# Moving the products, the split weights and one exponential around two RMSNorms of a two-layer trunk

## The chip, the cores and the metric

The kernel runs on one core of a Trainium2 chip. The core has a matrix engine (TensorE, PE, with a weight load PEld that overlaps it), a vector engine (VectorE, DVE), a scalar engine for activations and copies (ScalarE, ACT), a general engine (GpSimd, POOL) and a queue that issues the large transfers (SyncE, SP). Each engine works through its own instructions in order and waits for others by semaphores. The metric is the device time of one execution in microseconds (us): the median of the executions of one kernel. Lower is better.

## The reference

A trunk of two layers works on 256 tokens of width 2048 in float32. Layer 0 mixes tokens with a Conformer convolution, layer 1 with a Mamba-2 state-space mixer (64 heads in 8 groups); behind each mixer stands a squared-ReLU MLP with 8192 hidden columns. A norm with a modulation from a conditioning vector stands ahead of each of the four.

```python
for i in range(DEPTH):
    mod = (sc @ w_mod[i] + b_mod[i])[:, None, :]
    sh1, sc1, g1, sh2, sc2, g2 = jnp.split(mod, 6, axis=-1)
    u = rmsnorm(h, norm_mix_g[i]) * (1 + sc1) + sh1
    ...
    h = h + g1 * mix
    u = rmsnorm(h, norm_mlp_g[i]) * (1 + sc2) + sh2
    h = h + g2 * sq_relu_mlp(u, mlp_w1[i], mlp_w2[i])
return rmsnorm(h, final_norm_g)

def sq_relu_mlp(u, w1, w2):
    h = jax.nn.relu(u @ w1)
    return (h * h) @ w2

def mamba2(u, w_in, conv_w, conv_b, dt_bias, a_log, d_skip, norm_g, w_out):
    zxbcdt = u @ w_in
    z = zxbcdt[..., :D_INNER]
    xbc = zxbcdt[..., D_INNER:D_INNER + MB_CONV_CH]
    dt_raw = zxbcdt[..., D_INNER + MB_CONV_CH:]
    ...
    dt = jax.nn.softplus(dt_raw.astype(jnp.float32) + dt_bias.astype(jnp.float32))
    A = -jnp.exp(a_log.astype(jnp.float32)).reshape(MB_GROUPS, MB_HPG)
    y = ssd_chunked(xs, dt, A, Bm, Cm) + d_skip.reshape(MB_GROUPS, MB_HPG)[..., None] * xs
    ...

def ssd_chunked(xs, dt, A, Bm, Cm):
    ...
        acum = jnp.cumsum(dtc * a_f, axis=1)
        seg = acum[:, :, None] - acum[:, None, :]
        decay = jnp.exp(jnp.where(tril, seg, -jnp.inf))
    ...
```

## The kernel before

The stream `h` lies turned in the core's memory: columns of the model on the 128 partitions, the 256 tokens along a row, in four groups of four tiles (`h_75` to `h_78`). Weights come in blocks of 1 MB, issued by SP in the order of the program (`load_w`). Each weight and each activation is split into a high part of reduced precision and a low part that holds the rest: ACT casts the high part of half a block (`wh`, L386), DVE subtracts it to get the low part (`wl`, L388), both 128x1024. A product of full accuracy is then hi*hi + hi*lo + lo*hi. PE issues these as products of 512 columns (the high weight against both parts of the activation) and of 256 (the low weight), at L417, or at L401 as single products of 256.

**A norm.** Squares of `h` are taken on ACT as the last columns are added (`square_sum`, L599; the addition is L984). `rstd_cols` adds them over the partitions with products of one column (L573), ACT takes the root (L578) and DVE the reciprocal (L579). `rstd_bcast` puts the result on a diagonal (`diag`, L548) and PE spreads it over the partitions (L553). `modulate` then works on one tile of 128x256 after another: DVE multiplies (`nrm`, L607), ACT adds the shift and casts the high part of `u` (L537), DVE makes the low part (L538). The first product needs the first tile.

**Fill.** While PE has nothing to do in a norm, it is given products of constants (`turn`, `turn_over`, L561): 3 ahead of the column sums, 5 behind them, 6 ahead of the first product (`FILL`). Each shows as two records in the profile. Where `self.held` holds products that were set aside, `turn` issues those instead. This is so in the norm ahead of the first MLP; in the norms ahead of the mixer of layer 1 and of the second MLP it is empty.

**What sets the order.** A list scheduler places each instruction by the program's order and by priorities (`high_priority`), and `issue_after(x)` keeps an instruction behind `x` in the order of its engine. Inside `outer`, which opens an MLP with the products of several blocks in turn, the second half of the first weight is split behind the last square (`self.sq`) and the diagonal (`self.dg`).

**Time steps.** In the mixer, `time_steps` multiplies `u` with the columns of `w_in` for `dt` (L1268 and L1270, 16 pairs, placed between the first blocks of `w_in`), in two halves of split weights (L1262 and L1264). It then makes softplus, the exponential of `a_log` (`na`, L1285, negated at L1286) and the cumulative sums (scans, L1305). Those go to a buffer in device memory (`ac_d`), from which `scores` reads them back over all partitions (`acc`, L1345, issued by POOL) and adds the mask (L1351, on DVE). The sum of a block's products goes into `xpad` at L1198, by which a bank of PE's output comes free, and DVE's convolution works on `xpad` at L1218.

Of the kernel before, what the change touches and what calls it, by code (L numbers as in the profile page):

```python
# [15 lines left out]
P = 128  # L16
T = 256
# [41 lines left out]
OPEN = 3  # L59
# [3 lines left out]
FILL = 16, 3, 5, 6, 8  # L63

# [124 lines left out]
class Trunk:  # L189
# [303 lines left out]
    def outer(self, srcs, make, evac, pump, there=()):  # L493
# [3 lines left out]
        for _ in range(len(self.held) or 1):  # L497
            self.turn(banks[0][0][:, :P], FILL[4] if there else FILL[3])
        there = list(there)
        for g in range(4):  # L500
            x = make(g)
            for b, src in enumerate(srcs):
# [3 lines left out]
                with self.tc.high_priority(self.ahead):  # L506
                    after = (self.hi, self.split) if done else (self.sq, self.dg) if g == 0 and b == 0 else (None, None)
                    parts = self.split_w(w, done, after)
# [34 lines left out]
    def rstd_bcast(self, sums, n):  # L543

        nc = self.nc
        r = self.rstd_cols(sums, n, FILL[1])
# [5 lines left out]
        self.turn(ps[:, :P], FILL[2])  # L552
# [12 lines left out]
    def rstd_cols(self, sums, n, fill=0):  # L565
# [3 lines left out]
        if fill:  # L569
            self.turn(ps[:, :P], fill)  # L570
        for i, s in enumerate(sums):
            for q in range(2):
                ins = nc.tensor.matmul(ps[:, q:q + 1], lhsT=s[:, q * P:(q + 1) * P], rhs=self.ones[:, :1],  # L573
                                       start=i == 0 and q == 0, stop=i == len(sums) - 1, skip_group_check=True).ins
        if fill:
            self.pe = ins
# [25 lines left out]
    def modulate(self, r, layer, sc, sh, g):  # L602

        ug = self.b("u", [P, 4, 2 * T], F32R)
        for t in range(4):
# [4 lines left out]
            self.split = self.split_x(ug, t, m, self.mod_tile(layer, sh, g)[:, t:t + 1])  # L610
        return ug
# [425 lines left out]
    def mlp(self, layer, ss, pump=None, after=None, first=None):  # L1037
        nc, a = self.nc, self.a
        with self.tc.high_priority(AHEAD_CHAIN):
            r = self.rstd_bcast(ss, D)  # L1040
# [12 lines left out]
        for c in range(4):  # L1053
# [16 lines left out]
            if c == 0:  # L1070
                self.outer([a["w1"][layer, b] for b in range(OPEN)], make, act, first or (lambda g: 0))
                if layer == 1:
                    self.todo.append(self.to_rows())
# [90 lines left out]
    def mamba(self, ss):  # L1164
# [10 lines left out]
        self.time_steps(u)  # L1175
# [73 lines left out]
    def time_steps(self, u):  # L1249
# [6 lines left out]
        self.turn_over(bank[:, :P], FILL[3], self.pe)  # L1256
        for i in range(2):
# [5 lines left out]
            with self.tc.issue_after(self.dg) if i else nullcontext():  # L1263
                nc.vector.tensor_tensor(out=wl, in0=w[:, s8, :], in1=wh.bitcast(F32), op=ALU.subtract)  # L1264
            for k in range(8):
                kt = 8 * i + k
                x = u[kt // 4]
                nc.tensor.matmul(bank, lhsT=wh[:, k, :], rhs=x[:, kt % 4, :], start=kt == 0, stop=False,  # L1268
                                 skip_group_check=True)
# [14 lines left out]
        with self.tc.issue_after(self.sq):  # L1284
# [196 lines left out]
```

## Time and profile before

| what | before |
| --- | --- |
| median of 3 runs | 2544.52 us (2544.44 to 2545.41) |
| the profiled execution, its own time | 2543.68 us |
| its span in the profile | 2541.9 us |
| granted clock of PE, mean | 0.998 |
| DVE, low parts of weights (L388) | 940.9 us in 768, 1230 ns each |
| ACT, high parts of weights (L386) | 806.4 us in 768, 1051 ns each |
| DMA | 664.31 MB, 261 GB/s mean |

The times of the profile count from the start of the span. The norm ahead of the mixer stands at 1110 us, the one ahead of the second MLP at 1812 us. In the timeline `x6` counts records that follow each other, and the name in brackets behind an arrow is what ended the idle time ahead of the row. Matmuls are pipelined, so that the length of one record is more than the distance to the next.

### The profile page before, as it was taken

Reading aid. Unit: us, or ns where it says so; the run is one execution under the profiler, and the core shown is the slowest. Engines: PE = TensorE matmul, PEld = TensorE weight load, DVE = VectorE, ACT = ScalarE, POOL = GpSimd, SP = SyncE. Lnnn points to the kernel's source line nnn. Section 1 sums busy time; section 2 is a strip of 40 time slices with the busy share of each in tenths; the row PEclk is TensorE's granted clock in tenths of the full one; section 3 lists DMA queues with packets and bytes.
Section 4 is the critical chain, followed back from the end, with each engine's and each line's share of the span. In section 5 each row is a group of like instructions: output and inputs, shape, how many; then the busy total and the mean of one; then the engine's idle time right before and its main releaser. Section 6 shows DMA issues by size and latency. Waiting matters only on the chain.

```text
span 2541.9 us, 36894 instructions
## 1 busy us (share of the span) xinstructions
PE 2514.0 (99%) x14623; PEld 2170.2 (85%) x14623; DVE 1938.1 (76%) x2524; ACT 1326.4 (52%) x2030; POOL 145.1 (6%) x201
## 2 busy tenths in 40 slices
PE   9999999999999999999999999999999999999998
PEld 7888799988888888887888888888998888888887
DVE  6799888868878888887787878898975565565565
ACT  2088654544434434457777767744454443443444
POOL 0011000000100000001000000000001101001000
PEclk9999999999999999999999999999999999999999
DMA  9998887888888878856555455788765555555554
GB/s 403 419 354 290 346 353 288 292 339 311 322 310 330 330 309 332 311 199 205 190 193 184 171 187 188 253 321 320 284 249 198 185 196 187 195 186 196 191 191 149
DMA packets 94894, 664.31 MB, mean 261 GB/s; under 512 B 10977, under 2 KB 11105, under 8 KB 16769
## 3 DMA queue, kind: packets, MB, share of 16 engines
q1 hardware_dynamic: 89138, 643.82, 68.1%
q0 software_dynamic: 5152, 16.97, 2.4%
q8 instruction: 114, 1.87, 0.3%
q10 hardware_dynamic: 432, 1.19, 0.1%
q14 instruction: 58, 0.48, 0.1%
HBM read 656.50 MB, written 2.20 MB: 259 GB/s over the span
## 4 chain that ended last, share of the span: by engine, by line
PE 89%; DVE 5%; DMA 3%; ACT 2%; issue 1%; POOL 0%; SPq 0%; DVEq 0%; ACTq 0%; POOLq 0%
PE mm L417 49%; PE mm L401 11%; PE mm L460 8%; PE mm L461 8%; PE mm L459 8%; DVE taps L688 2%; DMA hid<-wmT 2%; ACT taps L670 1%; DVE hid L316 1%; PE mm L792 1%; PE ms L1404 1%; DMA w<-open 1%; DMA wm<-wmT 1%; DVE wm L316 1%; DMA acc<-ac_d 0%
## 5 line engine op out<-in xcount | busy, mean ns | idle before, releaser
L388 DVE TENSOR_TENSOR wl<-w,wh 128x1024 fp32r<-128x1024 f32 x768 | 940.9, 1230 | 476.3 <-ACT wh L386 471.9
L386 ACT CAST wh<-w 128x1024 fp32r<-128x1024 f32 x768 | 806.4, 1051 | 929.3 <-PE mm L417 476.3
L417 PE MATMUL mm<-u,wh 128*128 128x512 f32 x3136 | 995.8, 399 | 5.5 <-DVE xpad L1198 5.3
L417 PEld LDWEIGHTS mm<-u,wl 128*128 128x128 f32 x3136 | 588.4, 188 | 139.1 <-DVE wl L388 1.1
L417 PE MATMUL mm<-u,wl 128*128 128x256 f32 x3136 | 617.5, 278 | 0.6 <-DVE wl L388 0.6
L417 PEld LDWEIGHTS mm<-u,wh 128*128 128x128 f32 x3136 | 480.4, 189 | 13.6 <-DVE xpad L1198 5.8
L459 PE MATMUL mm<-wh,hid 128*128 128x512 f32 x896 | 350.7, 391 | 0.0
L461 PE MATMUL mm<-wh,hid 128*128 128x512 f32 x896 | 348.7, 389 | 0.0
L460 PE MATMUL mm<-wl,hid 128*128 128x512 f32 x896 | 348.6, 389 | 0.0
L316 DVE SCALAR_TENSOR_TENSOR wm<-wm,scb 128x2048 f32<-128x2048 f32 x134 | 306.4, 2287 | 15.1 <-DMA wm<-wmT 14.8
L401 PE MATMUL mm<-u,wh 128*128 128x256 f32 x1408 | 254.0, 284 | 0.8 <-DVE u L538 0.8
L401 PEld LDWEIGHTS mm<-u,wh 128*128 128x128 f32 x1408 | 218.4, 192 | 3.8 <-DVE u L538 1.2
L459 PEld LDWEIGHTS mm<-wh,hid 128*128 128x128 f32 x896 | 168.2, 188 | 35.6 <-issue 1.0
L460 PEld LDWEIGHTS mm<-wl,hid 128*128 128x128 f32 x896 | 168.2, 188 | 35.3 <-issue 0.5
L461 PEld LDWEIGHTS mm<-wh,hid 128*128 128x128 f32 x896 | 168.2, 188 | 35.0
L401 PE MATMUL mm<-u,wl 128*128 128x256 f32 x704 | 196.3, 283 | 0.3 <-DVE wl L388 0.2
L417 PE MATMUL mm<-hid,wh 128*128 128x512 f32 x448 | 141.9, 398 | 0.0
L401 PEld LDWEIGHTS mm<-u,wl 128*128 128x128 f32 x704 | 133.8, 192 | 0.7 <-DVE wl L388 0.7
L316 DVE SCALAR_TENSOR_TENSOR hid<-hid,scb 128x2048 f32<-128x2048 f32 x46 | 105.4, 2290 | 19.8 <-DMA hid<-wmT 19.8
L670 ACT ACTIVATE taps<-u,par 128x256 f32<-128x256 f32 x248 | 102.4, 501 | 8.6 <-DVE u L660 5.1
L417 PEld LDWEIGHTS mm<-hid,wl 128*128 128x128 f32 x448 | 84.1, 188 | 19.7
L345 POOL TENSOR_TENSOR mod<-mod,par 128x4 f32<-128x4 f32 x40 | 38.9, 972 | 1059.3 <-DVE wm L316 898.4
(264 smaller groups left out, 2206.1 us busy)
## 6 DMA issues: line engine op xcount, KB each, us to landing
w<-w SPq DMA_DIRECT2D x256, 1024.0 KB, 4.9
wm<-wmT SPq DMA_DIRECT2D x139, 1024.0 KB, 7.3
w<-win SPq DMA_DIRECT2D x80, 1024.0 KB, 4.9
hid<-wmT SPq DMA_DIRECT2D x53, 1024.0 KB, 11.0
w<-wout SPq DMA_DIRECT2D x32, 1024.0 KB, 6.7
w<-pw SPq DMA_DIRECT2D x27, 1024.0 KB, 5.5
w<-open SPq DMA_DIRECT2D x16, 1024.0 KB, 14.1
acc<-ac_d POOLq DMA_DIRECT2D x16, 512.0 KB, 8.4
```

What stands on the lines that cost most here:

```text
L316: self.sum = nc.vector.scalar_tensor_tensor(out=w, in0=w, scalar=1.0, in1=self.scb, op0=ALU.mult, op1=ALU.mult, accum_out=m[:, i:i + 1]).ins
L345: nc.gpsimd.tensor_tensor(out=m, in0=m, in1=b, op=ALU.add)
L386: nc.scalar.copy(out=wh, in_=w[:, s, :])
L388: nc.vector.tensor_tensor(out=wl, in0=w[:, s, :], in1=wh.bitcast(F32), op=ALU.subtract)
L401: self.pe = self.nc.tensor.matmul(out, lhsT=lhsT, rhs=rhs, skip_group_check=True, **kw).ins
L417: self.pe = self.nc.tensor.matmul(out, lhsT=lhsT, rhs=rhs, start=start and not lows, stop=stop and bool(lows), skip_group_check=True).ins
L459: mm(banks[q], lhsT=hi, rhs=wh[:, k, :], start=t == 0, stop=False)
L460: mm(banks[q], lhsT=hi, rhs=wl[:, k, :], start=False, stop=False)
L461: mm(banks[q], lhsT=lo, rhs=wh[:, k, :], start=False, stop=t == NT - 1)
L670: st["tap"] = nc.scalar.activation(out=p4[:, q, :], in_=vp[:, k + q:k + q + T], func=AF.Identity, scale=self.col("w_dw", ct * TAPS + k + q ...
L688: nc.vector.tensor_add(wide, wide, products(four("wl"), k))
L792: self.pe = nc.tensor.matmul(o, lhsT=w[:, i, j * P:(j + 1) * P], rhs=u[g][:, t, :], start=ct == 0 and j < 2, stop=ct == NT - 1, skip_group ...
```

## The change

In the two norms with an empty `self.held`, the column sums stand directly behind the last products of the block ahead; the 5 fills behind the sums become 3 (`AFTER_SUMS`), the 6 ahead of the first product 4 (`TO_FIRST`). The first weight of an MLP is loaded and its first half is split ahead of the norm's chain, the low part behind the last addition to `h` (`self.evac`); the high part of the second half stands behind the last square and its low part behind the split of the second tile of `u` (`self.second`). In the mixer, the low part of the second half of the time steps' weights is placed behind the last split of the first group of `u` instead of the diagonal, and the exponential of `a_log` behind the last high part of that group instead of the last square. The first product of the time steps is issued in two halves, the one with the high parts first.

```diff
 FILL = 16, 3, 5, 6, 8
+AFTER_SUMS, TO_FIRST = 3, 4
...
-    def outer(self, srcs, make, evac, pump, there=()):
+    def outer(self, srcs, make, evac, pump, there=(), hi_after=None):
...
-            self.turn(banks[0][0][:, :P], FILL[4] if there else FILL[3])
+            self.turn(banks[0][0][:, :P], FILL[4] if hi_after is None else FILL[3] if self.held else TO_FIRST)
...
-                    after = (self.hi, self.split) if done else (self.sq, self.dg) if g == 0 and b == 0 else (None, None)
+                    after = (None, None) if not done else (hi_after, self.second) if hi_after else (self.hi, self.split)
...
-        r = self.rstd_cols(sums, n, FILL[1])
+        r = self.rstd_cols(sums, n, FILL[1], True)
...
-        self.turn(ps[:, :P], FILL[2])
+        self.turn(ps[:, :P], FILL[2] if self.held else AFTER_SUMS)
...
-    def rstd_cols(self, sums, n, fill=0):
+    def rstd_cols(self, sums, n, fill=0, chain=False):
...
-        if fill:
+        if fill and self.held:
             self.turn(ps[:, :P], fill)
-        for i, s in enumerate(sums):
-            for q in range(2):
...
+        with self.tc.issue_after(self.pe) if chain else nullcontext():
+            for i, s in enumerate(sums):
+                for q in range(2):
...
-        if fill:
+        if chain:
             self.pe = ins
...
             self.split = self.split_x(ug, t, m, self.mod_tile(layer, sh, g)[:, t:t + 1])
+            if t == 1:
+                self.second = self.split
...
     def mlp(self, layer, ss, pump=None, after=None, first=None):
         nc, a = self.nc, self.a
+        w = self.load_w(a["w1"][layer, 0][0])
         with self.tc.high_priority(AHEAD_CHAIN):
+            half = self.split_half(w, 0, None, self.evac)
             r = self.rstd_bcast(ss, D)
...
-                self.outer([a["w1"][layer, b] for b in range(OPEN)], make, act, first or (lambda g: 0))
+                self.outer([a["w1"][layer, b] for b in range(OPEN)], make, act, first or (lambda g: 0),
+                           there=[(w, [half])], hi_after=self.sq)
...
-        self.time_steps(u)
+        self.time_steps(u, rows)
...
-        self.turn_over(bank[:, :P], FILL[3], self.pe)
+        self.turn_over(bank[:, :P], TO_FIRST, self.pe)
...
-            with self.tc.issue_after(self.dg) if i else nullcontext():
+            with self.tc.issue_after(first[1]) if i else nullcontext():
                 nc.vector.tensor_tensor(out=wl, in0=w[:, s8, :], in1=wh.bitcast(F32), op=ALU.subtract)
...
-                nc.tensor.matmul(bank, lhsT=wh[:, k, :], rhs=x[:, kt % 4, :], start=kt == 0, stop=False,
-                                 skip_group_check=True)
+                for c in (slice(0, T), slice(T, 2 * T)) if kt == 0 else (slice(0, 2 * T),):
+                    nc.tensor.matmul(bank[:, c], lhsT=wh[:, k, :], rhs=x[:, kt % 4, c],
+                                     start=kt == 0 and c.start == 0, stop=False, skip_group_check=True)
...
-        with self.tc.issue_after(self.sq):
+        with self.tc.issue_after(first[0]):
             nc.scalar.activation(out=na, in_=self.col("a_log", 0)[:H], func=AF.Exp)
```

The lines of the kernel move by up to 9, so that L388 becomes L389, L538 L539, L607 L610, L1264 L1272 and L1351 L1360. The number behind a name counts buffers and differs by a few between the two kernels.

DVE in the norm ahead of the mixer, before, from the reciprocal on (`wl_9604` is the low part of the time steps' second half, `wl_9684` that of the mixer's first block, `u_9506` and `u_9523` the first two groups):

```order
L579 RECIPROCAL rcol_9494<-rcol_9494 128x2
L548 TENSOR_TENSOR diag_9497<-ident,rcol_9494 128x256
L1264 TENSOR_TENSOR wl_9604<-w_1432_9574,wh_9603 128x1024
L607 SCALAR_TENSOR_TENSOR nrm_9507<-h_75,mod_5089,ms_9499 128x256
L607 SCALAR_TENSOR_TENSOR nrm_9511<-h_75,mod_5089,ms_9499 128x256
L1286 TENSOR_SCALAR na<-na 64x1
L538 SCALAR_TENSOR_TENSOR u_9506<-nrm_9507,mod_6136,u_9506 128x256
```

and, seven rows further on:

```order
L607 SCALAR_TENSOR_TENSOR nrm_9524<-h_76,mod_5390,ms_9499 128x256
L607 SCALAR_TENSOR_TENSOR nrm_9528<-h_76,mod_5390,ms_9499 128x256
L388 TENSOR_TENSOR wl_9684<-w_1449_9681,wh_9683 128x1024
L538 SCALAR_TENSOR_TENSOR u_9523<-nrm_9524,mod_6412,u_9523 128x256
L538 SCALAR_TENSOR_TENSOR u_9523<-nrm_9528,mod_6412,u_9523 128x256
```

The same place of DVE in the changed kernel, where the first `nrm` follows the diagonal at once (left out), from the second group on:

```order
L610 SCALAR_TENSOR_TENSOR nrm_9519<-h_76,mod_5390,ms_9496 128x256
L610 SCALAR_TENSOR_TENSOR nrm_9523<-h_76,mod_5390,ms_9496 128x256
L1272 TENSOR_TENSOR wl_9598<-w_1432_9569,wh_9597 128x1024
L539 SCALAR_TENSOR_TENSOR u_9518<-nrm_9519,mod_6412,u_9518 128x256
L539 SCALAR_TENSOR_TENSOR u_9518<-nrm_9523,mod_6412,u_9518 128x256
L610 SCALAR_TENSOR_TENSOR nrm_9527<-h_76,mod_5390,ms_9496 128x256
L610 SCALAR_TENSOR_TENSOR nrm_9531<-h_76,mod_5390,ms_9496 128x256
L1295 TENSOR_SCALAR na<-na 64x1
L389 TENSOR_TENSOR wl_9678<-w_1449_9675,wh_9677 128x1024
```

The time steps' low part, the constant and the first block's low part have all moved behind the first group. On PE the 16 pairs of time-step products then end with fewer block products between them (38 of 512 and 38 of 256 before, 32 and 30 now).

DVE at the first scores, 60 us further on, before (`acc` is the tile that waits for the read of `ac_d`, `xpad` what a bank of PE's output waits for):

```order
L388 TENSOR_TENSOR wl_10117<-w_1520_10114,wh_10116 128x1024
L1218 SCALAR_TENSOR_TENSOR a_9882<-xpad,par,a_9882 128x256
L1351 TENSOR_TENSOR acc_9927<-acc_9927,mask 128x1024
L1351 TENSOR_TENSOR acc_9928<-acc_9928,mask 128x1024
L388 TENSOR_TENSOR wl_10121<-w_1520_10114,wh_10120 128x1024
L1198 TENSOR_TENSOR xpad<-mm_9893,lo_10071 128x256
```

and in the changed kernel:

```order
L1360 TENSOR_TENSOR acc_9921<-acc_9921,mask 128x1024
L389 TENSOR_TENSOR wl_10037<-w_1505_10030,wh_10036 128x1024
L1360 TENSOR_TENSOR acc_9922<-acc_9922,mask 128x1024
L389 TENSOR_TENSOR wl_10111<-w_1520_10108,wh_10110 128x1024
L389 TENSOR_TENSOR wl_10115<-w_1520_10108,wh_10114 128x1024
L1206 TENSOR_TENSOR xpad<-mm_9887,lo_10065 128x256
```

The masks have moved up past the splits of one and a half blocks.

DVE in the norm ahead of the second MLP, before (`wl_16314` and `wl_16372` are the low parts of the first two weights):

```order
L984 SCALAR_TENSOR_TENSOR h_78<-mm_15996,mod_8059,h_78 128x256
L579 RECIPROCAL rcol_16265<-rcol_16265 128x2
L548 TENSOR_TENSOR diag_16268<-ident,rcol_16265 128x256
L388 TENSOR_TENSOR wl_16314<-w_2497_16307,wh_16313 128x1024
L607 SCALAR_TENSOR_TENSOR nrm_16291<-h_75,mod_8358,ms_16270 128x256
L607 SCALAR_TENSOR_TENSOR nrm_16295<-h_75,mod_8358,ms_16270 128x256
L388 TENSOR_TENSOR wl_16372<-w_2502_16365,wh_16371 128x1024
L538 SCALAR_TENSOR_TENSOR u_16290<-nrm_16291,mod_14542,u_16290 128x256
```

and in the changed kernel (`wl_16250` is the low part of the first half of the first weight, `wl_16301` that of its second half):

```order
L989 SCALAR_TENSOR_TENSOR h_78<-mm_15990,mod_8059,h_78 128x256
L389 TENSOR_TENSOR wl_16250<-w_2481_16247,wh_16249 128x1024
L582 RECIPROCAL rcol_16262<-rcol_16262 128x2
L549 TENSOR_TENSOR diag_16265<-ident,rcol_16262 128x256
L610 SCALAR_TENSOR_TENSOR nrm_16284<-h_75,mod_8358,ms_16267 128x256
L610 SCALAR_TENSOR_TENSOR nrm_16288<-h_75,mod_8358,ms_16267 128x256
L539 SCALAR_TENSOR_TENSOR u_16283<-nrm_16284,mod_14536,u_16283 128x256
```

Nothing stands any more between the diagonal and the first split of `u`; the first weight's low part is ahead of the reciprocal.

More of the change, by code (lines that the diff above doesn't have):

```diff
@@ L563, in turn_over @@
         return ins
-    def rstd_cols(self, sums, n, fill=0):
+    def rstd_cols(self, sums, n, fill=0, chain=False):
         nc = self.nc
         ps = self.bank(self.ms, "ms")
-        if fill:
+        if fill and self.held:
             self.turn(ps[:, :P], fill)
-        for i, s in enumerate(sums):
-            for q in range(2):
-                ins = nc.tensor.matmul(ps[:, q:q + 1], lhsT=s[:, q * P:(q + 1) * P], rhs=self.ones[:, :1],
-                                       start=i == 0 and q == 0, stop=i == len(sums) - 1, skip_group_check=True).ins
-        if fill:
+        with self.tc.issue_after(self.pe) if chain else nullcontext():
+            for i, s in enumerate(sums):
+                for q in range(2):
+                    ins = nc.tensor.matmul(ps[:, q:q + 1], lhsT=s[:, q * P:(q + 1) * P], rhs=self.ones[:, :1],
+                                           start=i == 0 and q == 0, stop=i == len(sums) - 1,
+                                           skip_group_check=True).ins
+        if chain:
             self.pe = ins
@@ L1247, in mamba, with time_steps @@
         return st["ss"]
-    def time_steps(self, u):
+    def time_steps(self, u, first):
         nc, a = self.nc, self.a
```

## The prediction

> **What bounds the kernel now.** I read the page first, then what TensorE (PE) waited for, then the chain of waits and the timeline around the norms that the change touches.
>
> ```profile
> span 2541.9 us, 36894 instructions
> PE 2514.0 (99%) x14623; PEld 2170.2 (85%) x14623; DVE 1938.1 (76%) x2524; ACT 1326.4 (52%) x2030; POOL 145.1 (6%) x201
> ```
>
> PE is busy 99% of the span, so a cut on any other engine is worth only the PE idle time or the PE filler that it takes away. The waits of PE, longest in total first (line waited at, what released it, us in total, times, longest):
>
> ```profile
> PE mm L417 <- DVE xpad L1198: 5.3, 1, 5.3
> ...
> PE mm L716 <- DVE u L660: 1.6, 1, 1.6
> ...
> PE mm L401 <- DVE u L538: 0.8, 2, 0.6
> ...
> PE mm L417 <- DVE wl L388: 0.6, 1, 0.6
> ```
>
> The 5.3 us lie 40 us behind the mixer's norm, where the first scores are masked. The small ones at L401, L1268 and `wl` lie in the norms; there PE's time hides in filler (L561), which counts as busy. So the views that decide are the chain at the two norms and at that 5.3 us gap. The first MLP's norm is not part of the sum: with products still in `self.held` its branches are those of before, and its rows stand in the same order on every engine.
>
> **Norm ahead of the second MLP.** Chain of waits, start, length, what:
>
> ```profile
> 1812.45 0.67 PE ms L561 x6
> 1813.12 1.68 PE ms L573 x16
> 1814.80 1.22 PE ms L561 x10
> 1816.02 0.44 PE ms L1102 x4
> 1816.46 0.45 PE ms L553 x2
> ...
> 1817.33 0.47 DVE nrm L607
> 1817.80 1.14 DVE wl L388
> 1818.94 0.41 DVE u L538
> ...
> 1819.39 10.69 PE mm L401 x87
> ```
>
> and two rows of the timeline there:
>
> ```profile
> 1813.33 1.03 ACT L386 CAST wh<-w 128x1024 fp32r<-128x1024 f32 x1
> 1814.84 0.26 ACT L578 ACTIVATE rcol<-ms,eps 128x2 f32<-128x2 f32 x1 [0.48 <-PE ms L573]
> ```
>
> Three fills (six records) ahead of the sums go, so the sums start at 1812.45 and end at 1814.13, 0.67 earlier. The root cannot follow by all of it: the cast on ScalarE (ACT) runs to 1814.36, so it gains 0.48. PE's 3 fills (0.73) and 4 transposes (0.44) behind the sums end at 1815.30, about when `diag` is ready, so the broadcast starts near 1815.35 instead of 1816.46. The first `nrm` gains 1.0 (VectorE, DVE, is now held by `diag` and the broadcast). The `wl` of 1.14 between `nrm` and the low part of `u` is gone from that place, 0.2 of this is lost to ACT's high part: the low part starts at 1816.94 instead of 1818.85 and the first product that waits for it at 1817.46 instead of 1819.39. That is **1.9 us**. What is late next: the second half's `wl`, behind the second split; it ends before PE reaches it, since PE has 4 chunks of products with the first half (over 2 us) ahead. Behind 1819.39 PE runs without a gap, so the 1.9 us reach the end.
>
> **Norm ahead of the mixer.** The same edits, another result. Rows of its chain and of the timeline:
>
> ```profile
> 1110.50 0.67 PE ms L561 x6
> ...
> 1118.78 0.78 DVE nrm L607 x2
> 1119.56 1.14 DVE wl L388
> ...
> 1120.75 0.74 PE mm L417 x4
> 1121.49 0.23 PE mm L1268
> ...
> 1122.20 1.17 PE mm L417 x7
> 1123.37 0.23 PE mm L1268
> ```
>
> ```profile
> 1113.16 1.28 ACT L1285 ACT_TABLE_LOAD   x1
> 1113.72 1.22 DVE L1264 TENSOR_TENSOR wl<-w,wh 128x1024 fp32r<-128x1024 f32 x1
> 1116.58 0.50 PE L1268 MATMUL mm<-u,wh 128*128 128x512 f32 x1 [0.69 <-DVE u L538]
> ```
>
> The sums again start 0.67 earlier; `wl` of L1264 (1.22) is no longer ahead of `nrm`, the table load and the constant are no longer ahead of ACT's first high part, and the first product needs only the high part. I get it at 1115.19 instead of 1116.58: 1.39 gained. But nothing is removed from DVE, only moved behind, and here DVE sets the pace. Group 0's last split ends at 1117.9 (0.9 earlier); behind it come two `nrm` (0.78), the moved `wl` (1.14) and the fifth low part (0.41 in the chain above), so PE gets that at 1120.3, having run out at 1118.9. Then the sixth low part, two `nrm`, the constant and the block's `wl` (0.4 + 0.8 + 0.1 + 1.14) end at 1122.7. By then PE has done 6 pairs of time-step products (0.35 each: 0.23 for L1268 here and 0.12 for L1270 in the fence below) and 8 block products of 512 (seven products of L417, three of 512 and four of 256, took 1.17, so 0.23 and 0.12 each): 3.96 us of work in 7.49. Before it had done 5.59 us of work (6 pairs, 11 of 512, 8 of 256) by 1123.37. It will have the missing 1.63 done at 1124.31, 0.94 later than before; small waits that remain in the rows of before come off, and I take **0.7 us later**. This norm gives its gain back.
>
> **The time steps and the gap of 5.3 us.** The time steps' last product ended at 1137.25 in the chain; from there through the scans to the DMAs and the mask:
>
> ```profile
> 1137.13 0.12 PE mm L1270
> ...
> 1158.03 0.27 DVE wm L1305
> ...
> 1158.59 3.62 DMA ac_d<-wm
> ...
> 1163.42 10.73 DMA acc<-ac_d
> ...
> 1174.17 0.04 DVE acc L1351
> ...
> 1175.32 1.22 DVE wl L388
> 1176.54 0.34 DVE xpad L1198
> ...
> 1176.92 8.24 PE mm L417 x37
> ```
>
> ```profile
> 1137.17 1.05 ACT L386 CAST wh<-w 128x1024 fp32r<-128x1024 f32 x1 [1.83 <-PE mm L1268]
> ...
> 1170.89 1.22 DVE L1351 TENSOR_TENSOR acc<-acc,mask 128x1024 f32<-128x1024 f32 x1 [4.27 <-DMA acc<-ac_d]
> ```
>
> ```profile
> 1176.88:1180.15 3.27, 3.23 (x10) 2.75 (x11) 2.21 (x4) 2.40 (x8) 0.00 (x0) 0.50 1.03 343
> ```
>
> ```profile
> 275.70:279.00 3.30, 3.29 (x59) 2.34 (x63) 2.12 (x3) 1.61 (x4) 0.00 (x0) 1.00 1.03 429
> ```
>
> Between the first and the last time-step product stood 38 block products of 512 and 38 of 256; now it is 32 and 30. That is 6 x 0.23 + 8 x 0.12 = 2.3 us earlier; less the 0.7 of the norm, 1.6. ACT's copy of the result stood behind the cast of the row at 1137.17, which ended 0.97 us after the product; that cast now falls elsewhere among the products, which I put at 0.6; between there and the scans two convolution steps fewer stand on DVE. So the scans end 2.0 to 2.3 us earlier, and with the same DMA times (3.62, 10.73) both parts of `acc` arrive some **2.0 us earlier**: near 1168.8 and 1172.1.
>
> At the gap the row that PE waits for is `xpad` (L1198), and in front of it on DVE stand the mask additions, which wait for those DMAs. Before, one `wl` (1.22) stood between the second mask and `xpad`; now two do, and the first mask has moved ahead of another one. Behind the waiting masks are queued all of DVE's low parts, and PE waits for these. The second mask starts at 1172.1, and mask, `wl`, `wl` and `xpad` take 1.15 + 1.14 + 1.14 + 0.38: PE is at this row near 1176.0 instead of 1176.92, a gain of **0.9**. Its wait is no longer one of 5.29 us: it should fall into one of about 2.2 (to a `wl` behind the first mask) and two near 0.5.
>
> The last two fences (window, length, busy time of PE, PEld, DVE, ACT, POOL with counts, granted clock, DMA share, GB/s) show the clock at 0.50 for 3.27 us behind the gap, so half of that, 1.6 us, is lost; and at 1.00 behind the wait of 1.6 us at L716, which ended at 275.7. With waits of 2.2 at most I take the clock as kept: **1.6 gained**. A page speaks against taking fills out and against this step: the Trainium skill, "TensorE: Matmul & The Clock Gate", Part 1 (The HAM clock gate), has the clock halved after an idle window of about 3.4 us that runs freely. The 0.50 for 3.27 us behind a 5.29 us gap agrees with it; by that rule a gap of 2.2 us would keep the clock, two gaps that share a window might not.
>
> **Other edits.** SP and POOL issue in the same order as before, so no DMA passes another one; the exponential's table load (1.28) meets ACT while it has slack, between 0 and 1.28 late for one high part, and I take 0, since DVE is behind ACT there. Splitting one product of 512 (0.23) into two of 256 (0.12 each) costs nothing.
>
> **Sum.** -1.9 + (-0.9) + (-1.6) = -4.4; the 0.7 and the 2.3 are inside the 0.9. The profiled execution took 2543.68 us, so 2539.3 is forecast for such a one. The median of the runs, 2544.52, lies 0.84 higher, so **2540.1**.
>
> **Rivals.** (1) The clock closes all the same, in the gap (2.2 lies between the 1.6 that kept it and the 5.3 that lost it) or in the mixer's norm, where PE is busy 0.7 us between 1118.9 and 1122.7: 1.6 more, 2541.7. 18%. (2) The DMAs arrive as before, because a 1 MB weight load takes the DMA engines (share 1.03 in the row behind the gap) whenever the scans end: then the additional `wl` costs 1.1 at the gap and the clock falls as before. -1.9 + 1.1 = -0.8, 2543.7. 15%. (3) Slower: the read of `acc` is issued behind that weight load and takes 13 instead of 10.7 us (such reads took up to 13.1):
>
> ```profile
> DMA to landing us min/median/max: 4.8/8.4/13.1
> ```
>
> Each us of arrival is a us of PE; the kernel is slower than before from an arrival 0.8 us later than today's, and at 2 us later with all fills gone the sum is -1.9 + 1.1 + 2.0 = +1.2: 2545.7. 5%. (4) The arrival is over 3 us earlier, with a read of 8.4, the median: the gap nearly closes, 1.5 more, 2538.6. 15%. (5) The table load holds ACT for longer. The profile shows 1.28, started 0.02 after the root ended. If a switch cost twice that, the moved load would delay the fifth low part by 0.9 and all behind it: 2541.0. 5%. The Trainium skill, "ScalarE: Activation LUTs", What ACT_TABLE_LOAD costs, gives 1283 ns and a drain of 1380 ns, 2.66 us for a switch; no drain shows in the rows here.
>
> That the change does not do what it says is ruled out by the order of the rows shown with it.
>
> **How the numbers follow.** The forecast has 42%, with 2539.0 to 2541.3 of its own (mostly 0.7 in the mixer's norm either way). 0.2% (5.1 us) is about what a measurement of this kernel can tell from no change; faster by that means below 2539.43: rival 4 and about a third of the forecast's range, 28%. Slower by that is above 2549.6, beyond every case: 2%. The range of 8 in 10 reaches from 2537.9 (most of rival 4) to 2544.0 (rival 2), leaving out rival 3 and the edges.
>
> **What would show it.** In the profile after: the first waited product of the second MLP about 5.0 us behind the end of the block's products (6.9 before, 1812.45 to 1819.39); in the mixer's norm PE waiting about 1.4 us for `u` and 1.6 for `wl`; the write of `ac_d` about 2 us earlier against the norm's start; a wait for `xpad` under 1 us, one of 2 us a little earlier, and a granted clock of 1.00 there. A clock of 0.50 is rival 1, an unmoved arrival rival 2. The forecast is wrong where PE waits at a place that none of this names.

## The result, and the profile after

The changed kernel takes 2538.63 us (median of 9 runs, 2537.0 to 2539.75) and the kernel before 2544.86 us (9 runs, 2544.42 to 2545.66): a ratio of 0.9973 with a 95% interval of 0.9965 to 0.9981. It is 6.2 us faster, where 4.4 were forecast; the time lies in the range, 1.5 us below the forecast. The profiled execution took 2537.33 us.

The page of the changed kernel, its waits of PE and the chain of waits where the long gap was:

```profile
span 2535.5 us, 36834 instructions
...
PE 2509.7 (99%) x14596; PEld 2166.1 (85%) x14596; DVE 1937.3 (76%) x2524; ACT 1320.2 (52%) x2026; POOL 145.1 (6%) x201
```

```profile
PE mm L797 <- ACT u L791: 4.4, 12, 0.8
PE mm L251 <- DMA wm<-crow: 3.0, 1, 3.0
PE mm L721 <- DVE u L665: 1.8, 1, 1.8
...
PE mm L418 <- DVE wl L389: 1.4, 1, 1.4
...
PE mm L1277 <- DVE u L539: 1.2, 1, 1.2
```

```profile
1158.58 4.27 PE mm L418 x23
1162.85 0.49 PE ms L1343 x4
1163.34 0.11 PE ms L1348
1163.45 19.04 PE mm L418 x109
```

The wait of 5.3 us for `xpad` is gone altogether: through the first scores the chain is PE alone. In its place stand 1.2 and 1.4 us in the norm ahead of the mixer. VectorE and POOL show why (timeline; in brackets what ended the idle time):

```profile
1167.70 1.23 DVE L1360 TENSOR_TENSOR acc<-acc,mask 128x1024 f32<-128x1024 f32 x1 [2.83 <-DMA acc<-ac_d]
1168.84 1.22 DVE L389 TENSOR_TENSOR wl<-w,wh 128x1024 fp32r<-128x1024 f32 x1
1169.97 1.22 DVE L1360 TENSOR_TENSOR acc<-acc,mask 128x1024 f32<-128x1024 f32 x1
1171.11 2.35 DVE L389 TENSOR_TENSOR wl<-w,wh 128x1024 fp32r<-128x1024 f32 x2
1173.38 0.75 DVE L1206 TENSOR_TENSOR xpad<-mm,lo 128x256 f32<-128x256 f32 x2
```

The second mask no longer waits at all: its data was there before 1169.97 (its read was issued at 1160.68 and took 9.0 us).

To compare executions, the profiles are cut at two marks: A is the start of the last addition to `h` ahead of the mixer's norm, C that ahead of the second MLP's norm. These are the rows for A, of before and of after:

```profile
1110.54 0.48 DVE L984 SCALAR_TENSOR_TENSOR h<-mm,mod,h 128x256 f32<-128x256 f32 x1 [0.23 <-PE mm L401]
```

```profile
1112.12 0.48 DVE L989 SCALAR_TENSOR_TENSOR h<-mm,mod,h 128x256 f32<-128x256 f32 x1 [0.23 <-PE mm L402]
```

For C they start at 1812.49 and 1807.80. So A to C took 701.95 and 695.68 us (**-6.27**), C to the end 729.41 and 727.70 (**-1.71**), and up to A, where both kernels run the same rows, the profiled execution of after was 1.58 us slower. The table holds all kernels by these marks; times of rows are starts after A, the scans' is their end, and all are differences of rows of the profiles.

| kernel | first product | scans end | reads issued | masks 1, 2 | wait for `xpad` | A to C | C to end |
| --- | --- | --- | --- | --- | --- | --- | --- |
| before | 6.04 | 47.75 | 51.95 | 60.35, 63.63 | 5.3 | 701.95 | 729.41 |
| changed | 4.74 | 45.10 | 47.66 | 55.58, 57.85 | none | 695.68 | 727.70 |
| wl back | 4.93 | 47.16 | 51.28 | 59.35, 63.81 | 6.1 | 702.48 | 727.80 |
| exponential back | 5.00 | 45.33 | 47.88 | 55.89, 58.17 | none | 695.97 | 727.75 |
| fills back | 5.26 | 45.63 | 48.18 | 56.08, 58.36 | none | 696.21 | 728.83 |
| mixer's edits alone | 5.78 | 45.61 | 48.17 | 56.06, 58.34 | none | 696.15 | 729.41 |
| load held | 6.04 | 47.80 | 51.14 | 61.47, 66.04 | 7.7 | 704.44 | 729.40 |
| two hops | 5.39 | 47.04 | 56.91 | 65.15, 66.95 | 5.9 | 705.83 | 727.79 |
| order alone | 5.39 | 48.12 | 51.87 | 59.01, 61.99 | none | 694.81 | 727.73 |
| wl ahead of norm | 5.11 | 47.19 | 51.25 | 57.74, 62.92 | 5.1 | 702.38 | 727.68 |
| one hop | 4.74 | 45.12 | 49.95 | 56.69, 58.48 | 0.3 | 696.93 | 727.76 |
| wl early, exponential late | 4.80 | 47.62 | 51.26 | 58.53, 61.91 | none | 694.33 | 727.64 |

The stretch from C to the end agrees within 0.2 us among the kernels that are alike there, so it resolves tenths where the whole times, which spread by 0.4 to 5 us for one kernel, do not. From A to C this holds only between profiles in which the granted clock ran alike, and that differs by execution. In the mixer's norm the clock stood at 0.50 for 3.41 us in the profiles of experiments 6 to 9, from 2.6 to 3.5 us after A on, and in experiment 6 once more from 12.9. Experiment 6 (window, length, busy times of PE, PEld, DVE, ACT, POOL, granted clock, DMA share, GB/s):

```profile
1113.40:1116.80 3.40, 3.21 (x12) 2.89 (x13) 1.77 (x5) 1.31 (x3) 0.00 (x0) 0.50 0.00 0
1123.65:1127.05 3.40, 3.40 (x14) 3.11 (x15) 2.40 (x5) 2.27 (x3) 0.00 (x0) 0.50 0.37 152
```

The profile of the changed kernel has 1.00 at both places, though its rows up to 44 us after A stand in the same order as those of experiments 6 and 9. In experiment 6 the first product is therefore 0.65 and the end of the scans 1.94 us later than in the changed kernel before any copy is made. Of the eight profiles with less filler four show such a fall, of the four with the filler of before (before, 3, 4, 5) none; twelve executions do not settle whether the filler decides it.

### The profile page after: what moved, and what is told of

Same layout as the page of the kernel before. It is cut to its first block, busy times and chain, and to the rows that moved or that the text cites. A ratio compares the mean times of both kernels' runs of the same rounds, so it can differ in the third digit from the quotient of the medians.

```text
span 2535.5 us, 36834 instructions
## 1 busy us (share of the span) xinstructions
PE 2509.7 (99%) x14596; PEld 2166.1 (85%) x14596; DVE 1937.3 (76%) x2524; ACT 1320.2 (52%) x2026; POOL 145.1 (6%) x201
## 4 chain that ended last, share of the span: by engine, by line
PE 89%; DVE 5%; DMA 3%; ACT 2%; issue 1%; SPq 0%; POOL 0%; DVEq 0%; ACTq 0%; POOLq 0%
PE mm L418 49%; PE mm L402 11%; PE mm L460 8%; PE mm L462 8%; PE mm L461 8%; DMA hid<-wmT 2%; DVE taps L693 2%; ACT taps L675 1%; PE mm L797 1%; DVE hid L317 1%; PE ms L1413 1%; DMA wm<-wmT 1%; DVE wm L317 1%; PE ms L797 0%; DVE taps L687 0%
## 5 line engine op out<-in xcount | busy, mean ns | idle before, releaser
L389 DVE TENSOR_TENSOR wl<-w,wh 128x1024 fp32r<-128x1024 f32 x768 | 940.2, 1229 | 474.1 <-ACT wh L387 469.4
```

Source lines behind the costliest of these rows:

```text
L389: nc.vector.tensor_tensor(out=wl, in0=w[:, s, :], in1=wh.bitcast(F32), op=ALU.subtract)
```

## The experiments

**1. One edit undone: the place of wl.**

```diff
-            with self.tc.issue_after(first[1]) if i else nullcontext():
+            with self.tc.issue_after(self.dg) if i else nullcontext():
                 nc.vector.tensor_tensor(out=wl, in0=w[:, s8, :], in1=wh.bitcast(F32), op=ALU.subtract)
```

> The changed kernel with one edit undone: the low part of the time steps' second half (wl) stands behind the diagonal again, as before. Theory A (the place of this wl sets how many block products lie between the time-step products, and so when the scans end and the reads of ac_d land): 38 and 38 block products lie between them again, the reads land after PE has run out, the wait for xpad of about 5 us and the half clock behind it return, only the second MLP's 1.7 us and some 0.7 us of the mixer's norm stay: 2542.0 to 2543.0. Theory B (the fills, the early sums or the exponential's place close the gap, not this wl): the gap stays closed, 2538.6 or less.

It took 2543.51 us (ratio to before 0.9995, 0.9986 to 1.0004). Its waits and its chain of waits:

```profile
PE mm L418 <- DVE xpad L1206: 6.1, 1, 6.1
```

```profile
1158.67 3.54 DMA ac_d<-wm
1162.22 0.28 issue
1162.50 0.94 POOL acc L1354
1163.44 11.57 DMA acc<-ac_d
```

The gap is back and the whole gain but that of the second MLP is lost; 38 and 38 block products stand between the time-step products, as theory A has it. The time is 0.5 us above its range; the clock stood at 0.50 for 4.3 us behind the gap, 1.0 us longer than before. In the changed kernel the place of this one subtraction carries the mixer's part.

**2. One edit undone: the place of the exponential.**

```diff
-        with self.tc.issue_after(first[0]):
+        with self.tc.issue_after(self.sq):
             nc.scalar.activation(out=na, in_=self.col("a_log", 0)[:H], func=AF.Exp)
```

> The changed kernel with one edit undone: the exponential of a_log with its table load stands behind the last square again. Theory A (its place matters only in the norm): the table load of 1.3 us and the 0.2 us of the exponential stand ahead of the first high part again, the first product comes 0.4 to 1.0 us later, the gap ahead of xpad stays closed: 2539.0 to 2539.6. Theory B (the exponential's place closes the gap): the wait of 5 us for xpad returns, 2543 or more.

2537.01 us (0.997, 0.9959 to 0.9982), below the changed kernel's median, which neither theory gave. By the stages it is 0.29 us slower from A to C, and its first product is 0.26 later. The whole times cannot resolve that; the gap stayed closed, so theory B falls.

**3. The filler as before.**

```diff
-        if fill and self.held:
+        if fill:
...
-        self.turn(ps[:, :P], FILL[2] if self.held else AFTER_SUMS)
+        self.turn(ps[:, :P], FILL[2])
...
-            self.turn(banks[0][0][:, :P], FILL[4] if hi_after is None else FILL[3] if self.held else TO_FIRST)
+            self.turn(banks[0][0][:, :P], FILL[4] if hi_after is None else FILL[3])
...
-        self.turn_over(bank[:, :P], TO_FIRST, self.pe)
+        self.turn_over(bank[:, :P], FILL[3], self.pe)
```

> The changed kernel with the filler as before in both norms (3 ahead of the sums, 5 behind, 6 ahead of the first product). Theory A: each norm's root is 0.5 us later, as the cast on ScalarE hides the rest of the 0.67, and all behind it shifts: +1.0 in sum, 2539.4 to 2539.9, the gap stays closed. Theory B (less filler is what brings the gain): 2542 or more. Theory C (the filler keeps the clock and costs nothing): 2538.6 or less.

2538.79 us (0.9977, 0.9968 to 0.9986): as a whole time it is nearest to theory C, but by the stages it is not, where A to C is 0.53 and C to the end 1.13 us longer than in the changed kernel (the clock stood at 1.00 in these norms in both profiles). So less filler and earlier sums are worth 1.7 us in two norms, more than theory A's 1.0, and the first weight's early split is worth the other 0.58 of the second MLP's norm (729.41 less 728.83).

**4. The mixer's edits alone**, put into the kernel before: the two places of experiments 1 and 2. The first product stays whole, other than the expectation says.

```diff
-            with self.tc.issue_after(self.dg) if i else nullcontext():
+            with self.tc.issue_after(first[1]) if i else nullcontext():
...
-        with self.tc.issue_after(self.sq):
+        with self.tc.issue_after(first[0]):
```

> The kernel before with only the mixer's edits (place of wl and of the exponential, first product in two halves), filler and second MLP as before. Theory A: the gap ahead of xpad closes and the clock stays at 1.00 behind it, the norm ahead of the mixer gives back about 0.7 to 1.2 us: 2544.9 - 6.9 + 1.2 = 2539.2 to 2539.8, and the norm of the second MLP is unchanged. Theory B (fills and sums first close the gap): no gain, 2544 to 2545.5.

2539.54 us (0.9979, 0.997 to 0.9988), A to C 5.80 us shorter than before, no wait for `xpad`, C to the end as before. Theory A. In the mixer experiment 3 differs from this by the first product in two halves: there it comes 0.52 us earlier after A, and A to C is the same within 0.1, so the two halves gain nothing here.

**5. Why the reads land so early: a load held back.** In the changed kernel the reads are issued 2.26 us behind the write of `ac_d`, before it was 3.90. Between the two, the load that SP issues near the write has changed sides. POOL and SP in the timeline of before:

```profile
1158.59 0.58 POOL L1315 DMA_DIRECT2D ac_d<-wm  x1 [55.86 <-DVE wm L1305]
...
1162.49 1.84 POOL L1345 DMA_DIRECT2D acc<-ac_d  x2 [0.86 <-DMA ac_d<-wm]
```

```profile
1157.01 6.64 SPq L372 DMA_DIRECT2D w<-win  x2
```

and of the changed kernel, where the two loads of the last row stand at 1153.74 and 1160.34:

```profile
1157.52 0.58 POOL L1324 DMA_DIRECT2D ac_d<-wm  x1 [53.21 <-DVE wm L1314]
...
1159.78 1.83 POOL L1354 DMA_DIRECT2D acc<-ac_d  x2 [1.14 <-DMA ac_d<-wm]
```

```profile
1153.74 6.92 SPq L373 DMA_DIRECT2D w<-win  x2
```

Each of the two loads near the write starts 0.03 us behind the end of a low part, the last reader of a block's weights, by which a buffer comes free: that of 1157.01 behind the first of these two rows (before), that of 1160.34 behind the second (changed). The first row stands ahead of the scans, the second behind them:

```profile
1155.77 1.21 DVE L388 TENSOR_TENSOR wl<-w,wh 128x1024 fp32r<-128x1024 f32 x1
1159.09 1.22 DVE L389 TENSOR_TENSOR wl<-w,wh 128x1024 fp32r<-128x1024 f32 x1
```

What moved while the write of before was under way, by queues (packets, MB, share of the engines), from 1158.6 to 1161.0 and from 1161.0 to 1162.6; q0 carries what POOL issues:

```profile
q1 hardware_dynamic: 109, 0.88, 95.0%
```

```profile
q0 software_dynamic: 64, 0.10, 20.0%
q1 hardware_dynamic: 23, 0.07, 10.4%
```

For 2.4 us behind its issue no packet of the write moved, only the load; in the changed kernel the write's first packet stands 1.2 us behind its issue. So the kernel before got one wait:

```diff
+            if g == 1 and getattr(self, 'hold', False):
+                self.stream(self.one.tile([1, 16], F32, tag='hold', name='hold'), self.ac_d[:1, :16])
             w = self.load_w(src[g])
...
         for blk in range(20):
+            self.hold = blk == 2
```

> The kernel before with one wait added: the weight load that SP issues at 1157.0, 1.6 us ahead of the write of ac_d, is held until that write has landed (SP issues a read of 64 bytes of ac_d ahead of it). Theory A (write and load share the DMA engines, and part of the earlier arrival in the changed kernel is that its load comes behind the write): from the issue of the write to the issue of the reads 2.3 us instead of 3.9, the reads land 1.6 us earlier, the wait for xpad falls from 5.3 to about 3.7: 2543.3 with the half clock behind it, 2541.7 without. Theory B (the load does not matter): 3.9 us as before, 2544.5 to 2545.5.

2546.27 us (1.0004, 0.9994 to 1.0013), no faster, and outside the ranges of both theories. The two queues and the masks on VectorE:

```profile
1160.16 0.58 POOL L1318 DMA_DIRECT2D ac_d<-wm  x1 [55.91 <-DVE wm L1308]
1162.67 0.54 POOL L1319 DMA_DIRECT2D eac_d<-wm  x1 [1.92 <-ACT wm L1315]
1163.20 1.83 POOL L1348 DMA_DIRECT2D acc<-ac_d  x2
```

```profile
1162.16 0.25 SPq L372 DMA_DIRECT2D hold<-ac_d  x1
1162.52 2.71 SPq L372 DMA_DIRECT2D w<-win  x2
```

```profile
1173.53 1.22 DVE L1354 TENSOR_TENSOR acc<-acc,mask 128x1024 f32<-128x1024 f32 x1 [5.34 <-DMA acc<-ac_d]
1178.10 1.22 DVE L1354 TENSOR_TENSOR acc<-acc,mask 128x1024 f32<-128x1024 f32 x1 [3.35 <-DMA acc<-ac_d]
```

The write is indeed down to 2.0 us (1160.16 to 1162.16, when SP's held read could start). But POOL's next row, a second write that waits for ScalarE, holds the reads 1.0 us longer, and now two loads are issued right beside them (1162.5 and 1164.9): the reads land at 1173.5 and 1178.1, 10.3 and 14 us behind their issue. Theory A had the write right and the reads wrong: with the loads beside them they took longer.

**6. Two hops: the reads made late in the changed kernel.**

```diff
         nc.gpsimd.dma_start(out=self.ac_d, in_=ac)
+        hop = self.dr.tile([H, T], F32, tag='hop0', name='hop0')
+        nc.gpsimd.dma_start(out=hop, in_=self.ac_d)
+        self.ac_d = hop
+        hop = self.dr.tile([H, T], F32, tag='hop1', name='hop1')
+        nc.gpsimd.dma_start(out=hop, in_=self.ac_d)
+        self.ac_d = hop
```

> The changed kernel with ac_d copied twice more from buffer to buffer in device memory ahead of the reads, nothing else. Each copy should take the 2.3 us that the changed kernel shows from the write's issue to the reads' issue, so the reads land some 4.5 us later, as in the kernel before. Theory A (the arrival of acc closes the gap): the wait for xpad is back at 4 to 5.5 us with half the clock behind it, 2543.5 to 2545.5. Theory B (the order of masks and splits on VectorE closes it, not the arrival): the gap stays closed or below 1.5 us, 2540 or less.

2546.11 us (1.0004, 0.9995 to 1.0013). Chain of waits, and the clock behind the gap (window, length, busy times of PE, PEld, DVE, ACT, POOL, granted clock, DMA share, GB/s):

```profile
1158.12 1.99 DMA ac_d<-wm
1160.11 0.28 issue
1160.38 2.09 DMA hop<-ac_d
1162.47 0.28 issue
1162.75 4.65 DMA hop<-hop
...
1180.09 0.34 DVE xpad L1206
```

```profile
1180.40:1183.70 3.30, 3.22 (x10) 2.74 (x11) 2.25 (x5) 2.40 (x8) 0.00 (x0) 0.50 0.92 295
```

The gap is back at 5.9 us, with the clock at 0.50, though the time steps' edit is there: theory A by its mechanism, with a time above its range, to which the clock in the norm adds. More than the reads changed, though: on VectorE the two masks stand directly behind each other with one `wl` ahead of `xpad`, as before, so this run alone does not tell late data from that order; experiment 9 does. The two copies move the same 64 KB; the second took 4.65 us where the first took 2.09. Between the two SP issued a load of 1 MB (1160.93) and POOL two reads of 128 KB (from 1161.07), so how much of the 2.6 us is the load's is not separated.

**7. The order** (named "order alone" in the table). wl is back as in experiment 1, so the scans end late; the exponential stands behind that of the time steps.

```diff
-            with self.tc.issue_after(first[1]) if i else nullcontext():
+            with self.tc.issue_after(self.dg) if i else nullcontext():
...
-        nc.scalar.activation(out=e, in_=e, func=AF.Exp)
+        ex = nc.scalar.activation(out=e, in_=e, func=AF.Exp).ins
         na = self.one.tile([H, 1], F32, tag="na", name="na")
-        with self.tc.issue_after(first[0]):
+        with self.tc.issue_after(ex):
```

> The changed kernel with the time steps' wl behind the diagonal as in the first experiment (so the reads land late again), and the exponential of a_log placed behind the exponential of the time steps, which needs no table load of its own. On VectorE the scheduler then puts xpad behind the first mask and ahead of the second. Theory A (the gap is the wait of xpad behind a mask whose data is late): xpad comes at the first mask's arrival plus 1.2, so the wait falls from 6.1 us to 0.5 to 1.5, the clock stays at 1.00, and without the lost time of the norm the kernel takes 2535.5 to 2538. Theory B (late data stalls PE at the next place anyhow): a wait of 4 us or more remains behind it, 2541 or more.

2535.55 us (0.9962, 0.9949 to 0.9974), faster than before, and A to C 0.87 us shorter than in the changed kernel. VectorE:

```profile
1170.17 1.22 DVE L1360 TENSOR_TENSOR acc<-acc,mask 128x1024 f32<-128x1024 f32 x1
1171.31 0.42 DVE L1206 TENSOR_TENSOR xpad<-mm,lo 128x256 f32<-128x256 f32 x1
1171.68 1.23 DVE L389 TENSOR_TENSOR wl<-w,wh 128x1024 fp32r<-128x1024 f32 x1
1172.82 0.42 DVE L1206 TENSOR_TENSOR xpad<-mm,lo 128x256 f32<-128x256 f32 x1
1173.15 1.22 DVE L1360 TENSOR_TENSOR acc<-acc,mask 128x1024 f32<-128x1024 f32 x1
```

Nothing waits for `xpad`: two of them now stand ahead of the second mask. Theory A. The order is not the only thing that moved, though. Neither mask waits for data here; these are the times from issue to landing of the first read (issued at 1163.03) and the second (1164.50):

```profile
DMA to landing us min/median/max: 4.6/4.6/4.6
DMA to landing us min/median/max: 8.1/8.1/8.1
```

So the data landed 56.5 and 61.4 us after A, against 60.4 and 63.6 before and 55.6 and 57.6 in the changed kernel: only the second part is late, and less so than before. By an estimate from these rows an `xpad` behind the second mask would have been done near 63.0 (61.4, 1.1 for the mask, 0.4 of its own) instead of 60.6. There are two ways out of the gap, early data or an `xpad` that isn't queued behind the late data; the change took the first, and this run takes the second, with the first part of the data early as well.

**8. wl ahead of the norm.**

```diff
+        self.sqs = (getattr(self, "sqs", []) + [self.sq])[-4:]
...
-            with self.tc.issue_after(self.sq) if i else nullcontext():
+            with self.tc.issue_after(self.sqs[-3]) if i else nullcontext():
                 nc.scalar.copy(out=wh, in_=w[:, s8, :])
-            with self.tc.issue_after(first[1]) if i else nullcontext():
+            with self.tc.issue_after(self.evac) if i else nullcontext():
```

> The changed kernel with the time steps' second wl made ahead of the norm's chain: its high part behind the second of the last four squares, its low part behind the last addition to h, where VectorE waits for the root. Theory A (wl behind the first group costs PE 2.6 us of waits in the norm, but its late place keeps the time-step products together): the norm's waits for u and wl fall below 1 us, PE's order has 38 block products of 512 between the time steps again, the wait for xpad of 5 to 6 us returns: 2541.0 to 2542.5. Theory B (the gap depends on where DVE loses time in the norm, not on PE's order): it stays closed, 2536 to 2537.

2543.13 us (0.9991, 0.9983 to 1.0): somewhat above the 2541.0 to 2542.5 of theory A, but by its mechanism. PE's waits for `u` and `wl` in the norm are below 0.4 us, 38 block products of 512 lie between the time steps again, and the wait for `xpad` is 5.1 us.

**9. One hop**, as experiment 6 with a single copy.

```diff
+        hop = self.dr.tile([H, T], F32, tag='hop0', name='hop0')
+        nc.gpsimd.dma_start(out=hop, in_=self.ac_d)
+        self.ac_d = hop
```

> The changed kernel with ac_d copied once more ahead of the reads, to get a gap between none and 5.9 us. Theory A (PE waits for xpad behind the second mask, whose data is late): the reads are issued 2 to 3 us later than in the changed kernel, the second mask starts 3 to 5 us later, and the wait for xpad is 1.5 to 3.5 us. The clock behind it: at 1.00 by the forecast's step, and the kernel at 2540 to 2542; at 0.50 by the rival, another 1.6 us. Theory B (the changed kernel has several us of slack there): no wait for xpad, 2538 to 2539.

2539.01 us (0.9972, 0.996 to 0.9983). The reads are issued 2.3 us later, but they were shorter (6.7 and 7.6 us), so the second mask starts only 0.63 later, and the wait for `xpad` is 0.3; neither theory gave that. VectorE:

```profile
1167.30 1.23 DVE L1363 TENSOR_TENSOR acc<-acc,mask 128x1024 f32<-128x1024 f32 x1 [2.36 <-DMA acc<-hop]
1169.09 1.22 DVE L1363 TENSOR_TENSOR acc<-acc,mask 128x1024 f32<-128x1024 f32 x1 [0.56 <-DMA acc<-hop]
```

The masks stand directly behind each other here as in experiment 6 and in the kernel before, and with early data the gap is 0.3 instead of 5.9 us: it is the arrival that closes it, not the order of the masks. The changed kernel has some 0.3 us to spare there (0.63 less 0.3), not several. A to C is 1.25 us longer than in the changed kernel; this wait and a new one of 0.4 us at L1389 are part of that, the rest is open. What the clock does behind a gap of 2 to 3 us at this place was not answered.

**10. wl early and the exponential late**: the edits of 7 (the exponential) and 8 in one kernel.

```diff
-            with self.tc.issue_after(self.sq) if i else nullcontext():
+            with self.tc.issue_after(self.sqs[-3]) if i else nullcontext():
...
-            with self.tc.issue_after(first[1]) if i else nullcontext():
+            with self.tc.issue_after(self.evac) if i else nullcontext():
...
-        with self.tc.issue_after(first[0]):
+        with self.tc.issue_after(ex):
```

> The two last edits together, from the changed kernel: the time steps' second wl ahead of the norm's chain and the exponential of a_log behind that of the time steps. On VectorE xpad again stands ahead of the second mask. Theory A: no wait for xpad above 1 us, the clock at 1.00, the norm's waits of PE below 1 us in sum, so as fast as the kernel with the order alone or 0.5 us faster: 2534.8 to 2536. Theory B (the second wl ahead of the reciprocal holds the norm up): the first product 0.3 us later than in the kernel with the order alone and 0.5 to 1 us more in the mixer: 2536 to 2537.

2534.67 us (0.9955, 0.9941 to 0.9968), the fastest of all: about 11 us below the kernel before by its ratio (0.0045 of 2545). A to C is 0.48 us shorter than in experiment 7, as theory A has it (the time is 0.1 below its range), and the first product comes 0.59 earlier; but the clock fell in the norm of experiment 7's profile and not in this one, so how much of the 0.48 is the place of wl is not shown. As there, `xpad` passes the second mask, whose data is late.

## Why the forecast was right in its direction and short by 1.8 us

- **Norm ahead of the second MLP**, forecast -1.9: measured -1.71 (C to the end). The first product stands 4.62 us behind C and none waits long behind it, as the walk had it.
- **Norm ahead of the mixer**, forecast +0.7 with the first product 1.39 us earlier: it came 1.30 earlier (6.04 less 4.74), and at the same count of block products PE is 0.8 to 0.9 us later than before (the 101st after A stands at 31.57 instead of 30.73, the 261st, just ahead of the gap, at 61.12 instead of 60.23). PE's waits were forecast at 1.4 and 1.6 and are 1.2 for `u` and 1.4 for `wl`; VectorE sets the pace there, and the norm gives its gain back.
- **Scans**, forecast 2.0 to 2.3 us earlier, as 1.6 for the block products and 0.6 for the copy behind the last one: 2.65. The last time-step product comes 1.49 us earlier (24.94 instead of 26.43 after A), its copy is read 0.53 sooner behind it, and VectorE's steps from there to the end of the scans take 0.63 less, which had no number in the forecast. Experiment 1 takes 2.06 of the 2.65 away by its one edit.
- **Arrival of `acc`**, forecast 2.0 us earlier: this is the term that was mis-sized. The reads were issued 4.29 us earlier (51.95 less 47.66), the first mask started 4.77 us earlier, and the second part landed 6.0 us earlier. The step that failed reads "with the same DMA times (3.62, 10.73)": the write took 2.0 us, as the load ahead of it, issued 3.8 us before, was all but done, and the second read 9.0; why the read was shorter is not shown. With the scans' 2.65 these 1.6 and 1.7 make the 6.0. Why the load moved is in VectorE's order: the `wl` that frees the load's buffer now stands behind the scans. That was to be read from the order before the run, and I had compared SP's order alone, in which nothing moved, and not what SP's rows wait for. The step "no DMA passes another one" failed with it. Experiment 5 shows the load's part: 2.0 against 3.6 us for the write once the load is held, and reads of 10.3 and 14 us beside two loads.
- **Wait for `xpad`**, forecast from 5.3 to a few waits of 2.2 and less (-0.9): it closed. -5.3, less what PE came later to this place.
- **Clock**, forecast 1.6 us kept: right in its sum for the profiled execution, for a better reason than the one given, since no gap was left at `xpad`. In every kernel with a wait of 5.1 to 7.7 us the clock fell to 0.50 during the wait and stood there for 3.3 to 5.9 us behind it (3.25 before, 5.85 in experiment 8). The rule of the Trainium skill that the prediction cited, "TensorE: Matmul & The Clock Gate", Part 1 (The HAM clock gate), agrees with that.
- **Clock in the norm**, which the forecast left to rival 1: that rule of an idle window does not explain the first falls in the norm of experiments 6 to 9: in the 3.41 us ahead of each, PE's records leave no idle time above 0.4 us, and they hold the column sums; why the clock fell there is open. The second fall in experiment 6 is what the prediction said of two gaps that share a window: PE idled 1.1 and 1.4 us there with 1.0 us of work between, all changes of the clock in that trace (1113.40, 1116.81, 1123.64, 1127.05, 1178.25, 1185.08) lie whole multiples of 3.41 us apart, and the 3.41 us ahead of 1123.64 hold 2.3 us of that idle time. In the profile of the changed kernel the same two waits (1.2 and 1.4) left the clock at 1.00. So the place that rival 1 names in the mixer's norm is a real one, and the changed kernel meets it in some executions of these rows.
- **Exponential**, forecast at 0: its new place is worth 0.29 us by the stages, the first product's 0.26.
- **Sum**: -5.3 and -1.6 at the gap and the 0.9 by which PE comes later to it make -6.0 of the -6.27 from A to C; the other 0.3 is not traced. With -1.71 that is -8.0, and the 1.58 us by which that execution came later to A leave the -6.4 of the spans. Rival 4 (an arrival over 3 us earlier, with shorter reads) had the effect, at 2538.6, and the shorter read as part of the cause; the shorter write it did not have. In this profile neither rival 1 (a clock of 0.50) nor rival 2 (an unmoved arrival) shows.

How much of the -6.2 of the medians is the 1.58 us ahead of A is not settled: A stands between 1110.5 and 1112.3 in the twelve profiles, and kernels that are alike up to there differ as much as before and after do. Nor is the clock settled for the median: of the nine executions of the changed kernel the two with a mean clock of 0.999, the profiled one among them, took 2537.0 and 2537.3 us, the seven with 0.997 or 0.998 2537.1 to 2539.8. One fall of 3.41 us lowers the mean by 0.0007 and costs at most 1.7 us; where the clock fell in those seven is not on record.

## What to carry to other kernels

A long wait that ends in a transfer is worth tracing through both queues: what counts is which loads are issued next to it, and that hangs on the instruction that frees their buffers, on another engine. Look first at what is queued behind the waiting instruction: in experiments 7 and 10 two short additions stand ahead of the late mask, and PE waits for nothing there, though the second part of the data landed some 4 us later than in the changed kernel. And filler on the tensor engine that hides a wait is a cost of its own where the work behind it is ready (1.7 us in two norms); its worth shows by stages, not in whole times, and a profile in which the clock stayed up with less filler does not show that it always does.

## What the runs showed of the hardware

- A transfer of 64 KB took 2.0 to 2.1 us with no load issued in the 3.5 us ahead of it and 3.5 to 3.6 us when a load of 1 MB was issued 1.6 us ahead of it on another queue (before and experiment 1); the first two reads of 512 KB took 4.6 us (experiment 7) to 14 (experiment 5, beside two such loads). The Trainium skill, "DMA: Bandwidth & Descriptors", Queues, rings and completion order, has each engine take turns between queues by whole packets. Such turns do not show for the write of before: none of its packets moved from 1158.6 to 1161.0, while the load moved 0.88 MB.
- The granted clock of PE is 1.00 or 0.50 in the stretches shown, and a fall within the run lasts 3.41 or 6.83 us. Equal rows in equal order can meet it or not: the norm of the mixer in the changed kernel and in experiments 6 and 9.
- Executions of the same rows differ early: the first 1110 us, the same in all kernels, vary by 1.8 us between the profiles, and among PE's first waits is one for a transfer at the start (3.0 us in the changed kernel, 2.6 with one hop).
